# A ConvFFN's last product with one more folded pair of tiles in each half, and two of its weight sums made one stage earlier

## The chip, the cores and the metric

The kernel runs on one core of one Trainium2 chip. The metric is the device time of that core in microseconds: 1489.67 us before the change, the median of three runs that span 1489.61 to 1492.81. All traces quoted are of single executions on that core.

## What is computed

One layer of a diffusion backbone on 256 latent tokens of width 2048 and 256 context tokens: adaLN modulation, two attention branches, an output projection, and then a gated ConvFFN. The change concerns the end of it:

```python
def conv_ffn(h, w_up, conv_w, conv_b, w_down):
    u = depthwise_conv(h @ w_up, conv_w, conv_b)
    a, g = jnp.split(u, 2, axis=-1)
    return (jax.nn.silu(g) * a) @ w_down
...
y = (jax.nn.sigmoid(ga) * (oa @ w_br_a) + jax.nn.sigmoid(gb) * (ob @ w_br_b)) @ w_o
x = x + gt1 * rms_norm(y, g_attn_post[l])
h = modulate(rms_norm(x, g_ffn_pre[l]), sh2, sc2)
x = x + gt2 * rms_norm(conv_ffn(h, w_up[l], conv_w[l], conv_b[l], w_down[l]), g_ffn_post[l])
```

`w_up` is 2048 x 11264, `w_down` is 5632 x 2048: 44 tiles of 128 rows, called ff tiles below. All weights and activations are fp32.

## The kernel before

**Products.** Every fp32 product is made of three matmuls on fp32r halves: each operand is split into a high and a low part, and high·high, low·high and high·low are added in PSUM. Weights arrive by DMA in blocks of 128 x 2048 fp32 (1 MB, tiles `raw...`, a ring of four buffers, issued by SP in program order, line 154). `split` makes the high part on ScalarE (L161, tiles `wh`) and the low part, raw minus high, on VectorE (L165, tiles `wl`); each has two buffers. One such pass covers 1024 columns, so a block takes two.

**The last product** is w_down's, made in two halves `h` of 1024 output columns, each of two column blocks of 512, for two blocks of 128 tokens. Its blocks come in the order of the string `SEQ`, once per half:

- `D`, a plain block: four 128 x 512 weight tiles, each times two token blocks, three matmuls each: 24 matmuls of 128x512 (`direct`).
- `S`, a folded pair of ff tiles (`fold`). Two tiles by two column blocks by two token blocks are eight products; with sums and differences of weights and of activations seven are enough, so 21 matmuls stand for 24. The four products on sums of weights use `t0h`, `t0l`, `t1h`, `t1l`; the three on the weights themselves use `wh`, `wl`. Results that belong to several outputs stay in PSUM as x1, x5, x6, x7 and are added at the end of the half (`sums_1`, `sums_2`).

Each half has 10 D and 12 S. A fold needs, beside 0.75 MB of its own weights (loads of L204, 128x512 and 128x1024), a 1 MB tile of weight sums. `weight_sums` (L239, L241, L242) makes it in place, in three VectorE operations on a raw block. For 22 of the 24 folds this happens in the up stage, beside the w_up product: `load_sum` loads the raw block, `sum_part` sums it, and POOL's DMA queue stores the tile to DRAM (`sumd`, L279). In the last product SP loads it back (L154, `raw<-sumd`). For pair 0 of each half the fold loads its full raw block and sums it itself, beside the last product (`folded`).

**Activations.** The gated activations of plain ff tiles stay split in `ff`. Those of a folded pair are summed by `act_sums` (L263) and split into `fs`, if they are kept; for the pairs in `LATE` the unsummed activations stay in `late_a` and are summed and split anew into `late_f` in each half. The up stage ends with the evacuation of its last product (L313, L314), a three-tap convolution (L1434, L1435, L1437) and the gate (L1442, L1445).

**Wo's end.** Before the FFN, the output projection Wo runs in four column blocks c of several weight blocks g; `beside(c, g)` hangs extra work behind each. Its products are L1164, evacuation and norm sums L1173, L1174, L1245, L1250, L1251, the residual L1263.

**What sets the order.** The program is written in one order, and a scheduler places each engine's instructions in its own in-order queue; `issue_after` ties an instruction behind another one. `block(n)` splits the next block of weights and loads n blocks ahead. TensorE, VectorE, ScalarE and SP then each work through a fixed list, and wait for semaphores.

## Time and profile before

| | |
|---|---|
| median of three runs | 1489.67 us (1489.61 to 1492.81) |
| the profiled execution: its own time | 1490.08 us |
| its span in the trace | 1488.2 us, 22084 instructions |
| last product, from its first to its last matmul's start | 1255.6 to 1480.0 us |
| Wo's end (last two column blocks) | about 700 to 763 us |
| granted TensorE clock | 1.00 nearly throughout |
| bytes moved | 446.11 MB, 300 GB/s on the mean |

The span is what the trace covers; the execution's own time is 1.9 us longer, and all sums below are made on it. The chain of waits tells which engine's work the end hung on; the list of groups tells durations by the form of the operand; the list of waits and the brackets in the timeline tell what an engine stood idle for. In the timeline a row reads: start, length, engine, line, operation, out<-in, and in brackets the idle time ahead of it with what ended it.

### The profile page before, as it was taken

The page shows a single profiled execution, that of the slowest core. Times are in us where ns is not written, and L with a number is a line of the kernel's source. Part 1 is how long each engine was busy: PE and PEld are TensorE (multiplying, and loading weights), DVE is VectorE, ACT ScalarE, POOL GpSimd, SP SyncE. Part 2 cuts the span into 40 slices and gives each one's busy share as a digit, 9 for nine tenths or more (in the row PEclk, how much of TensorE's full clock was granted, in tenths as well). Part 3 has the DMA queues.
Part 4 walks back from the last instruction along what each step waited for, and adds up shares of the span by engine and source line. Part 5 has one row for each costly group of instructions (what it writes and reads, how often), then busy time and mean ns, then how long its engine had stood idle before and what let it go on. Part 6 is the DMA issues. An engine that isn't in the chain of part 4 may idle for free.

```text
span 1488.2 us, 22084 instructions
## 1 busy us (share of the span) xinstructions
PE 1478.9 (99%) x8458; PEld 1273.1 (86%) x8458; DVE 1274.5 (86%) x1961; ACT 848.8 (57%) x1405; POOL 13.6 (1%) x33
## 2 busy tenths in 40 slices
PE   9999999999999999999999999999999999999998
PEld 7877889998888888888888888888888888788886
DVE  4499878889988989899878998898999998887886
ACT  5553324777764544555766555565555555675663
POOL 0000000000000000000000000000000000000000
PEclk9999999999999999999999999999999999999999
DMA  9988699754368898986646989989889888797794
GB/s 370 394 321 340 243 387 357 268 192 170 142 237 328 340 344 310 361 325 262 236 179 235 358 338 334 337 314 354 327 310 360 328 317 290 280 323 264 275 336 200
DMA packets 73688, 446.11 MB, mean 300 GB/s; under 512 B 7904, under 2 KB 10352, under 8 KB 25328
## 3 DMA queue, kind: packets, MB, share of 16 engines
q1 hardware_dynamic: 69840, 420.85, 75.8%
q0 software_dynamic: 3168, 23.07, 3.8%
q8 instruction: 66, 1.08, 0.3%
q10 hardware_dynamic: 576, 0.80, 0.2%
q14 instruction: 38, 0.31, 0.1%
HBM read 417.37 MB, written 27.32 MB: 299 GB/s over the span
## 4 chain that ended last, share of the span: by engine, by line
PE 94%; DVE 3%; ACT 1%; DMA 1%; issue 0%; ACTq 0%; DVEq 0%
PE pu L308 21%; PE pu L309 11%; PE c L1552 9%; PE pk L589 8%; PE pv L851 7%; PE pg L308 7%; PE pq L308 4%; PE pb L308 4%; PE x L1552 4%; PE pg L309 4%; PE py_o L1164 3%; PE pq L309 2%; PE pb L309 2%; PE po L993 1%; PE s L962 1%; PE o L1092 1%
## 5 line engine op out<-in xcount | busy, mean ns | idle before, releaser
L165 DVE TENSOR_TENSOR wl<-raw,wh 128x1024 fp32r<-128x1024 f32 (+1 forms) x444 | 514.6, 1186 | 90.2 <-ACT wh L161 88.1
L161 ACT ACTIVATE wh<-raw 128x1024 fp32r<-128x1024 f32 (+1 forms) x444 | 441.4, 1027 | 193.6 <-issue 53.9
L308 PE MATMUL pu<-h,wh 128*128 128x512 f32 x1404 | 487.6, 391 | 0.0
L309 PE MATMUL pu<-h,wl 128*128 128x256 f32 x1404 | 395.9, 282 | 0.0
L308 PEld LDWEIGHTS pu<-h,wh 128*128 128x128 f32 x1404 | 263.6, 188 | 55.0
L309 PEld LDWEIGHTS pu<-h,wl 128*128 128x128 f32 x1404 | 265.5, 189 | 0.0
L308 PE MATMUL pg<-h,wh 128*128 128x512 f32 x464 | 161.5, 390 | 0.0
L309 PE MATMUL pg<-h,wl 128*128 128x256 f32 x464 | 130.9, 282 | 0.0
L313 ACT ACTIVATE half_u<-pu 128x256 f32<-128x256 f32 x88 | 33.5, 382 | 154.0 <-PE pu L309 153.9
L338 DVE SCALAR_TENSOR_TENSOR raw<-raw,crb 128x2048 f32<-128x2048 f32 x48 | 109.6, 2284 | 10.1 <-DMA raw<-in_wm_b_dram 10.1
L589 PE MATMUL pk<-h,ku 128*128 128x512 f32 x480 | 117.4, 398 | 0.3
L308 PE MATMUL pq<-h,wh 128*128 128x512 f32 x304 | 108.9, 396 | 0.1
L589 PEld LDWEIGHTS pk<-h,ku 128*128 128x128 f32 x480 | 87.6, 188 | 23.6 <-issue 3.9
L308 PEld LDWEIGHTS pg<-h,wh 128*128 128x128 f32 x464 | 87.1, 188 | 18.2
L851 PE MATMUL pv<-wh,h 128*128 128x512 f32 (+1 forms) x384 | 101.6, 354 | 0.0
L1552 PE MATMUL c<-wh,ff 128*128 128x512 f32 x320 | 98.5, 389 | 0.0
L308 PE MATMUL pb<-h,wh 128*128 128x512 f32 x256 | 89.4, 391 | 0.0
L309 PEld LDWEIGHTS pg<-h,wl 128*128 128x128 f32 x464 | 87.7, 189 | 0.0
L309 PE MATMUL pq<-h,wl 128*128 128x256 f32 x304 | 85.5, 281 | 0.0
L851 PEld LDWEIGHTS pv<-wh,h 128*128 128x128 f32 x384 | 67.7, 189 | 10.1
L309 PE MATMUL pb<-h,wl 128*128 128x256 f32 x256 | 72.1, 282 | 0.0
L1552 PEld LDWEIGHTS c<-wh,ff 128*128 128x128 f32 x320 | 60.0, 188 | 12.4
(332 smaller groups left out, 2288.4 us busy)
## 6 DMA issues: line engine op xcount, KB each, us to landing
raw<-in_ws_dram SPq DMA_DIRECT2D x222, 1024.0 KB, 6.1
raw<-in_wm_b_dram SPq DMA_DIRECT2D x64, 1024.0 KB, 5.0
sumd<-raw POOLq DMA_DIRECT2D x22, 1024.0 KB, 4.7
raw<-sumd SPq DMA_DIRECT2D x22, 1024.0 KB, 6.8
raw<-in_wm_sc_dram SPq DMA_DIRECT2D x15, 1024.0 KB, 8.2
raw<-in_ws_dram SPq DMA_DIRECT2D x22, 512.0 KB, 6.0
raw<-in_wkt_dram SPq DMA_DIRECT2D x10, 1024.0 KB, 7.6
raw<-in_wm_sh_dram SPq DMA_DIRECT2D x8, 1024.0 KB, 8.5
```

Source lines behind the costliest of these rows:

```text
L161: a_ = nc.scalar.activation(hi, src, AF.Copy)
L165: v_ = nc.vector.tensor_tensor(out=lo, in0=src, in1=hi, op=ALU.subtract)
L308: nc.tensor.matmul(pt[:, :], wh[:, w], a, start=first and i == 0, stop=False, skip_group_check=True)
L309: nc.tensor.matmul(pt[:, :S], wl[:, w], a[:, 0], start=False, stop=last and i == n - 1, skip_group_check=True)
L313: a_ = nc.scalar.activation(t[:], pt[:, S:], AF.Copy)
L338: nc.vector.scalar_tensor_tensor(out=r, in0=r, scalar=1.0, in1=row, op0=ALU.mult, op1=ALU.mult, accum_out=modx[:, j : j + 1])
L589: nc.tensor.matmul(pk[:], wt[:, w], hh[:, :, k, a], start=k == 0 and a == 0 and wt is wh, stop=k == KT - 1 and a == 1)
L851: nc.tensor.matmul(pv[i][:, :nw], src[:, k, a, t0 : t0 + P], wt[:, w], start=k == 0 and q == 0, stop=k == KT - 1 and q == 2)
L962: nc.tensor.matmul(s_ps, qs[hd][:, a, qt * P : qt * P + P], k_[:, w], start=q == 0, stop=q == 2)
L993: nc.tensor.matmul(po[:, :S], v_[:, b], pTs[hd][:, b, a], start=b == 0 and q == 0, stop=b == 3 and q == 2)
L1164: p_ = nc.tensor.matmul(py[t][:], act[:, k, a, t * P : t * P + P], wt[:, w], start=k == 0 and q == 0, stop=k == nk - 1 and q == 2)
L1552: nc.tensor.matmul(pt[:], a(i), wt[:, w], start=k not in begun, stop=stop and q == 2, skip_group_check=True)
```

## The change

The last product has 13 folded pairs and 9 plain blocks a half instead of 12 and 10. The folded pairs begin at ff tile 14 instead of 16, so 18 instead of 20 ff tiles are plain and nine instead of eight summed pairs are kept in `fs`. The string starts with D S S and has three runs of S S S a half instead of two. Since 18 plain tiles make no whole number of blocks a column block, plain blocks take their (tile, column block) entries in one running list, and the fifth block of a half holds entries of both column blocks; the host lays the weights out so.

The pair that sums its own weights is now the last of each half (`OWN`), not the first. Its three products on its own weights come ahead of the four on sums, and the splits of its sums are placed inside the fold before it. The other 24 sums are made ahead: 22 in the up stage as before, and two more at Wo's end, hung into `beside`. Pads of the tiles `wh`, `wl`, of two small tiles and a 100-column tile `rim2` shrink or go, which makes room for `fs` and `ff`.

```diff
 NE = 6
 SW = (KT - ND) * P // 4
 KW = (NKVA + NHB) * P
-J0, NS = 16, 12
-ND0 = (FT - 2 * NS) // 4
-SEQ = "DDSSDSSDSSSDSSDSSSDDDD"
-LATE = (2, 4, 7, 9)
+J0, NS = 14, 13
+SEQ = "DSSDSSSDSSSDSSSDSSDDDD"
+LATE = (2, 5, 8, 11)
+OWN = (12,)
 PO = (2, 4, 6)
 KO = [j for j in range(KT) if j // 2 * 2 not in PO]
 SEQ_O = "DSDSDSDD"
-AHEAD = [(h, p) for h in range(2) for p in range(NS) if p not in (0,)]
+AHEAD = [(h, p) for h in range(2) for p in range(NS) if p not in OWN]
 NSUM = len(AHEAD)
 SUMS_UP = [3, *range(4, FT, 2), 37]
...
         n = r.shape[-1]
         b = 1 if pool else 2
         h, lo = (
-            (pool or wp).tile([P, 2048 + 128], F32R, tag=f"w{q}", bufs=b, name=f"w{q}{nraw[0]}")[:, off : off + 2048]
+            (pool or wp).tile([P, 2064], F32R, tag=f"w{q}", bufs=b, name=f"w{q}{nraw[0]}")[:, off : off + 2048]
             for q in "hl")
         def half(q, after):
             last[:] = split(h[:, q], lo[:, q], r[:, q], after)
...
     def folded(q):
 
         h, lo = (
-            wp.tile([P, 2048 + 128], F32R, tag=f"w{c}", bufs=2, name=f"w{c}{q}")[:, :2048] for c in "hl")
+            wp.tile([P, 2064], F32R, tag=f"w{c}", bufs=2, name=f"w{c}{q}")[:, :2048] for c in "hl")
         parts[q] = (h, lo), []
         after = tuple(sum_end) if SEQ[(q - b0 - B_DN - 1) % len(SEQ)] == "S" else None
         if q in sum_of and SEQ[(q - b0 - B_DN - 1) % len(SEQ)] == "D":
...
             wsum[q] = raws[q]
             for half in range(2):
                 weight_sums(raws[q], half)
-                split_sum(q, half)
+                if SEQ[(q - b0 - B_DN - 1) % len(SEQ)] == "D":
+                    split_sum(q, half)
 
     def weight_sums(r, part):
         q = [r[:, n * 512 : n * 512 + 512] for n in range(4)]
...
 
     def folded_o(q):
         r = raws[q]
-        h, lo = (wp.tile([P, 2048 + 128], F32R, tag=f"w{c}", bufs=2, name=f"w{c}{q}")[:, :2048] for c in "hl")
+        h, lo = (wp.tile([P, 2064], F32R, tag=f"w{c}", bufs=2, name=f"w{c}{q}")[:, :2048] for c in "hl")
         for w in (slice(0, 512), slice(1024, 2048)):
             split(h[:, w], lo[:, w], r[:, w])
         ts = []
         for i, c in enumerate("hl"):
             weight_sums(r, i)
-            t = place[b0 + B_UP - 1].tile([P, 2048 + 128], F32R, tag=f"w{c}", bufs=1, name=f"t{c}{q}")
+            t = place[b0 + B_UP - 1].tile([P, 2064], F32R, tag=f"w{c}", bufs=1, name=f"t{c}{q}")
             ts.append((t[:, :1024], t[:, 1024:2048]))
             queue[q + 1] = split(*ts[i], r[:, i * 1024 : i * 1024 + 1024])
         parts[q] = (h, lo), ts
...
         def beside(c, g):
             if c == 0 and g < 2:
                 sync.dma_start(out=x1[:, g], in_=xt[:, g])
+            if (c, g) in ((1, 3), (2, 1)):
+                load_sum()
+            if (c, g) in ((2, 0), (2, 2)):
+                with tc.issue_after(last[1]):
+                    sum_part(0)
+                    sum_part(1)
             if (c, g) == (2, 3):
                 nc.vector.tensor_tensor(
                     out=modx[:, 16:48], in0=modx[:, 16:48], in1=col[:, C_BMOD + 48 : C_BMOD + 80], op=ALU.add)
...
     yp = ctx.enter_context(tc.tile_pool(name="yp2", bufs=1))
     ss = yp.tile([P, 2, 4], F32, name="ss_2")
     r = yp.tile([P, 2], F32, name="r_2")
-    yp.tile([P, 100], F32, name="rim2")
     folding.append(yp)
     x1 = fs[:].rearrange("p k a i t -> p (k a i t)")[:, : 2 * D].bitcast(F32).rearrange("p (a d) -> p a d", a=2)
...
 
     row_of(0)
     down = [j for j in range(FT) if not is_folded(j)]
+    entries = [(j, c) for c in range(2) for j in down]
+    ndir = len(entries) // 4
     for h in range(2):
         c0, c1 = 2 * h, 2 * h + 1
         cs = [slice(c * 512, c * 512 + 512) for c in (c0, c1)]
...
                     pt[:], a(i), wt[:, w], start=k not in begun, stop=stop and q == 2, skip_group_check=True)
                 begun.add(k)
 
-        def direct(wts, g, c, t):
+        def direct(wts, d, t):
             for kk in range(4):
-                j = direct_tile(down[4 * g + kk])
+                n, c = entries[4 * d + kk]
+                j = direct_tile(n)
                 product(
                     C[t, c], lambda i: ff[:, j, i, t * P : t * P + P], *wts, slice(kk * 512, kk * 512 + 512), (t, c),
-                    stop=g == ND0 - 1 and kk == 3)
+                    stop=n == down[-1])
 
         def fold(wts, p, behind=None):
             (wh, wl), (ta, tb) = wts
...
             f_ = late_f if p in LATE else fs[:, kept(p)]
             A = lambda n: lambda i: f_[:, i, n]
             end = p == NS - 1
+            def plain():
+                product(X[1], A(0), wh, wl, sl[2], 1, end)
+                product(C[0, 0], A(1), wh, wl, sl[3], (0, 0))
+                product(C[0, 1], A(6), wh, wl, sl[0], (0, 1))
+
+            if p in OWN:
+                plain()
             product(X[7], A(5), *ta, sl[0], 7, end)
             product(X[5], A(3), *ta, sl[1], 5, end)
             if behind:
...
             product(C[1, 0], A(2), *tb, sl[1], (1, 0))
             if behind:
                 split_sum(behind, 1)
-            product(X[1], A(0), wh, wl, sl[2], 1, end)
-            product(C[0, 0], A(1), wh, wl, sl[3], (0, 0))
-            product(C[0, 1], A(6), wh, wl, sl[0], (0, 1))
+            if p not in OWN:
+                plain()
 
         def late_pair(p):
             return [late_a[:, LATE.index(p), q] for q in range(2)]
...
                         late[1:] = [lambda: (sums_2(), add(C[1, 1][:], C[1, 1][:], yg[:, 1, cs[1]]))]
             else:
                 for t in range(2):
-                    direct(wts, d % ND0, d // ND0, t)
+                    direct(wts, d, t)
                 d += 1
             if h and n == 4:
                 warm_table(AF.Sqrt, "d", ss[:, 0, 0:1])
...
             late = [lambda: None, scaled]
         else:
             wts, after = [], None
-            for g in range(ND0 - lead, ND0):
+            for g in range(ndir - lead, ndir):
                 wts.append(block(3))
-                direct(wts[-1], g, 1, 0)
-                close(g - ND0 + lead, 0, 1)
+                direct(wts[-1], g, 0)
+                close(g - ndir + lead, 0, 1)
             for t in range(2):
                 if t:
-                    for i, g in enumerate(range(ND0 - lead, ND0)):
-                        direct(wts[i], g, 1, 1)
+                    for i, g in enumerate(range(ndir - lead, ndir)):
+                        direct(wts[i], g, 1)
                 close(t, 1, 1 - t, after)
                 after = finish(t)
...
     ws[B_UP + 5 : B_DN : 2] = u[FT + 2 :]
     wd = f(w_down)[0].reshape(FT, P, D)
     down = [j for j in range(FT) if not is_folded(j)]
-    d = slabs(wd[down].reshape(-1, D), 512).reshape(2, 2 * ND0, P, 2048)
+    entries = [(j, c) for c in range(2) for j in down]
     for h in range(2):
-        n, g = iter(range(2 * ND0)), iter(range(NS))
+        n, g = iter(range(0, len(entries), 4)), iter(range(NS))
         for i, kind in enumerate(SEQ):
             if kind == "D":
-                ws[B_DN + h * len(SEQ) + i] = d[h, next(n)]
+                m = next(n)
+                ws[B_DN + h * len(SEQ) + i] = np.concatenate(
+                    [wd[j][:, h * 1024 + c * 512 : h * 1024 + c * 512 + 512] for j, c in entries[m : m + 4]], axis=1)
             else:
                 j = J0 + 2 * next(g)
                 a, b = (wd[k][:, h * 1024 : h * 1024 + 1024].reshape(P, 2, 512) for k in (j, j + 1))
```

Not shown are the same smaller pads in three further functions. Lines behind the first hunk move by 1 to 15: the sums are L240, L242, L243, the product is L1560.

**VectorE at Wo's end.** `wl179` to `wl184` are the low parts of Wo's last blocks, `raw179` and `raw182` now the raw blocks of the two sums; L1251 (now L1258) is the norm's sum. Before:

```order
L1111 TENSOR_TENSOR yg_6516<-o1_1_6532,yg_6516 128x512
L1128 TENSOR_TENSOR yg_6516<-yg_6516,grow_6517 128x512
L1251 SCALAR_TENSOR_TENSOR junk2_6523,sq_6519<-yg_6516,x1_6515 128x512
L1128 TENSOR_TENSOR yg_6516<-yg_6516,grow_6517 128x512
L1251 SCALAR_TENSOR_TENSOR junk2_6523,sq_6519<-yg_6516,x1_6515 128x512
L165 TENSOR_TENSOR wl179_6886<-raw178_6799,wh179_6885 128x1024 x2
L165 TENSOR_TENSOR wl180_6918<-raw179_6845,wh180_6917 128x1024 x2
L165 TENSOR_TENSOR wl181_6950<-raw180_6891,wh181_6949 128x1024 x2
```

Now:

```order
L1129 TENSOR_TENSOR yg_6518<-yg_6518,grow_6519 128x512
L240 TENSOR_TENSOR raw179_6839<-raw179_6839 128x1024
L1258 SCALAR_TENSOR_TENSOR junk2_6525,sq_6521<-yg_6518,x1_6517 128x512
L1129 TENSOR_TENSOR yg_6518<-yg_6518,grow_6519 128x512
L242 TENSOR_TENSOR raw179_6839<-raw179_6839 128x512
L1258 SCALAR_TENSOR_TENSOR junk2_6525,sq_6521<-yg_6518,x1_6517 128x512
L243 TENSOR_TENSOR raw179_6839<-raw179_6839 128x512
L165 TENSOR_TENSOR wl180_6894<-raw178_6801,wh180_6893 128x1024 x2
L165 TENSOR_TENSOR wl182_6928<-raw180_6849,wh182_6927 128x1024 x2
L240 TENSOR_TENSOR raw182_6925<-raw182_6925 128x1024
L165 TENSOR_TENSOR wl183_6964<-raw181_6899,wh183_6963 128x1024
L242 TENSOR_TENSOR raw182_6925<-raw182_6925 128x512
```

Three operations of the first sum stand ahead of the splits of one block of Wo, and those of the second stand among the splits of another.

**ScalarE where the up stage ends and the last product begins.** `half_u` and `a` belong to the last convolution, `wh312` (before) is the second plain block, `wh189` (before) and `wh188` (now) the first folded pair. Before:

```order
L313 ACTIVATE half_u87_12012<-pu43_1_11978 128x256
L161 ACTIVATE wh312_12031<-raw311_11914 128x1024
L1434 ACTIVATE a87_12015<-u87_12011,col_67 128x256
L161 ACTIVATE wh312_12031<-raw311_11914 128x1024
L1442 ACTIVATE a87_12015<-a87_12015 128x256
L161 ACTIVATE wh189_12077<-raw312_11968 128x512
L161 ACTIVATE ff_7469<-a43_11974 128x256
L161 ACTIVATE wh189_12077<-raw312_11968 128x1024
L161 ACTIVATE t0h189_12084<-raw312_11968 128x1024
L161 ACTIVATE t1h189_12090<-raw312_11968 128x1024
```

Now:

```order
L161 ACTIVATE wh188_12057<-raw314_11937 128x512
L314 ACTIVATE half_u87_12039<-pu43_1_12005 128x256
L161 ACTIVATE wh188_12057<-raw314_11937 128x1024
L1441 ACTIVATE a87_12042<-u87_12038,col_67 128x256
L1449 ACTIVATE a87_12042<-a87_12042 128x256
L161 ACTIVATE ff_7483<-a43_12001 128x256
L161 ACTIVATE t0h188_12059<-raw313_11935 128x1024
L161 ACTIVATE t1h188_12063<-raw313_11935 128x1024
```

The second plain block is gone from this place; the folded pair's own weights are split around the last evacuation, and `t0h`, `t1h` come from another raw tile than `wh`, the one loaded from DRAM.

**VectorE at the end of a half**, where the last pair (`204`) sums its own weights (`raw341`); `wl343` is the first of the four closing plain blocks. Now:

```order
L165 TENSOR_TENSOR wl204_12718<-raw341_12664,wh204_12717 128x512
L240 TENSOR_TENSOR raw341_12664<-raw341_12664 128x1024
L165 TENSOR_TENSOR wl204_12718<-raw341_12664,wh204_12717 128x1024
L165 TENSOR_TENSOR t0l204_12733<-raw341_12664,t0h204_12732 128x1024
L242 TENSOR_TENSOR raw341_12664<-raw341_12664 128x512
L243 TENSOR_TENSOR raw341_12664<-raw341_12664 128x512
L165 TENSOR_TENSOR wl343_12758<-raw342_12691,wh343_12757 128x1024 x2
L165 TENSOR_TENSOR t1l204_12743<-raw341_12664,t1h204_12742 128x1024
```

Before, the same operations stood at the head of a half; here a plain block's two splits come between the last sum and `t1l`.

More of the change, by code (lines that the diff above doesn't have):

```diff
@@ L341, in silu_row @@
     def silu_row(pool, tag="crb", bufs=1, v=0, like=F32):
-        r = pool.tile([P, D + (0 if like == F32 else 128)], like, tag=tag, bufs=bufs, name=f"crb{v}_{nmod[0]}")
+        r = pool.tile([P, D + (0 if like == F32 else 16)], like, tag=tag, bufs=bufs, name=f"crb{v}_{nmod[0]}")
         r = r if like == F32 else r[:, :D].bitcast(F32)
@@ L347, in gain_cols @@
     def gain_cols(i, j0, g0, pool):
-        g = pool.tile([P, 120], F32, tag="gr", bufs=1, name=f"gr{i}")[:, :KT]
+        g = pool.tile([P, KT], F32, tag="gr", bufs=1, name=f"gr{i}")
         nc.vector.tensor_tensor(
@@ L551, in unit @@
                     n, raw, o = 2 * NK2 * P, ru.pop(u), 0
-                h = wp.tile([P, 2048 + 128], F32R, tag="wh", bufs=2, name=f"ku{u}")[:, 8:]
+                h = wp.tile([P, 2064], F32R, tag="wh", bufs=2, name=f"ku{u}")[:, 8:]
                 step = 2 * P if u < 2 else n
```

## The prediction

> **What bounds the kernel now.** I read the share of busy time and the chain of waits first, then the last stage by itself.
>
> ```profile
> PE 1478.9 (99%) x8458; PEld 1273.1 (86%) x8458; DVE 1274.5 (86%) x1961; ACT 848.8 (57%) x1405; POOL 13.6 (1%) x33
> PE 94%; DVE 3%; ACT 1%; DMA 1%; issue 0%; ACTq 0%; DVEq 0%
> ```
>
> TensorE is busy in all but 1488.2 − 1478.9 = 9.3 us of the span, and 94% of the chain that ended last is its own work. So only two things can move the end: the number of matmuls, and the moments in which one of them waits. DVE at 86% is an average; what counts is whether a split is late for its matmul. The last stage, by the summary of the product's line and by two pieces of the chain (start, length, what, count):
>
> ```profile
> L1552 PE MATMUL c<-wh,ff x320: 388/389/396, 1255.6 to 1479.8; 128*128 128x512 f32 x160
> L1552 PE MATMUL c<-wl,ff x160: 388/389/393, 1256.0 to 1480.0; 128*128 128x512 f32 x160
> 1297.63 2.04 PE x L1552 x9
> 1457.25 23.13 PE c L1552 x102
> ```
>
> A record is 389 ns long, but they overlap: 102 of them take 23.13 us, 9 take 2.04, so one costs 0.2267 us of TensorE. The sequence has 2 × (10 plain × 24 + 12 folded × 21) = 984 matmuls: 223.1 us. From the first start to the end of the last at this pace pass 1480.0 + 0.2 − 1255.6 = 224.6 us, so some 1.5 us of the stage is waiting. Which waits, the list of waits in this stage says (total, times, longest):
>
> ```profile
> ACT t1h L161 <- DVE raw L242: 5.2, 2, 2.6
> ACT t0h L161 <- DMA raw<-sumd: 2.7, 3, 1.5
> PEld x L1552 <- ACT t1h L161: 0.9, 2, 0.5
> PEld x L1552 <- DVE t0l L165: 0.7, 1, 0.7
> PEld x L1552 <- DVE t1l L165: 0.5, 2, 0.3
> PE x L1552 <- DVE t0l L165: 0.2, 1, 0.2
> ```
>
> The waits for t1h and t1l come twice: pair 0 sums its own weights at the head of each half, and ScalarE stands 2.6 us for that sum. The waits for t0l belong to one late load of a sum from DRAM in half 0 (the chain has 8.85 us of it, shown below). The four rows of PEld and PE add up to 2.3 us, more than the 1.5 that PE can have lost, because a weight load may wait while the array still works. I scale them to 1.5: the two own sums cost 0.9 us, 0.45 a half, and the late load 0.6.
>
> **Fewer matmuls.** 13 folded pairs and 9 plain blocks a half are 273 + 216 = 489 matmuls, before 492. Six fewer over both halves, at 0.2267 us: **−1.36 us**. That is the whole arithmetic gain, and it is certain as far as PE is the bound. The Trainium skill ("TensorE: Matmul & The Clock Gate", section "Back-to-back issue gap") has about 131 ns sustained for 512 columns and 216 ns isolated; by these the six are worth an estimated 0.79 or 1.29 us. This trace's 226.7 ns agrees with neither, and nothing below uses them.
>
> **The own sum leaves the head of a half.** Pair 0 now reads its sum from DRAM in both halves. Half 1's head: its loads can run during the four plain blocks that end half 0, which are 4 × 24 × 0.2267 = 21.8 us of cover against 6.8 us for a load (rows below). Its stall goes: **−0.4**. Half 0's head is different: the sequence now starts with D S instead of D D S, so the first fold starts 5.44 us earlier against the last up products. Rows of before at that place on ScalarE (start, length; in brackets the idle time before it and what ended it):
>
> ```profile
> 1255.81 0.38 ACT L313 ACTIVATE half_u<-pu 128x256 f32<-128x256 f32 x1 [1.02 <-PE pu L309]
> 1260.42 0.42 ACT L1442 ACTIVATE a<-a 128x256 f32<-128x256 f32 x1 [1.84 <-DVE a L1437]
> 1261.53 0.40 ACT L161 ACTIVATE ff<-a 128x256 fp32r<-128x256 f32 x1
> 1263.91 1.06 ACT L161 ACTIVATE t0h<-raw 128x1024 fp32r<-128x1024 f32 x1 [1.03 <-DVE raw L239]
> 1267.60 1.06 ACT L161 ACTIVATE t1h<-raw 128x1024 fp32r<-128x1024 f32 x1 [2.62 <-DVE raw L242]
> ```
>
> PE ends its single plain block at 1255.6 + 5.44 = 1261.0, and by the new order then has three matmuls on this pair's own weights (to 1261.7), four on t0h, one more, one on t1h, two on t0l, three on t1h, then t1l. In the new order of ScalarE t0h stands right behind the last gate's L1442 and ff. With no plain block's splits in between, the chain (each step its predecessor's end and the length of its row in this place) half_u 1256.5, u 1257.3, wl 1258.7, the convolution's two steps 1259.6, gate 1260.0, product 1260.5, ff 1260.9 gives t0h at about 1261.9, t1h 1262.9, t0l 1263.1, t1l 1264.3. Needed, if PE does not stop before: 1261.7, 1262.8, 1263.1, 1264.2. So t0h is 0.2 late and the rest then fits; the next pair's t0l (1267.4) and t1l (1268.6) are just in time. I take 0.3 us. Below that bound is 0; above, if wl and the convolution change places on VectorE (1.2 us), 1.5. Against 0.45 before: **−0.1** (−0.4 to +1.1).
>
> The late load of half 0, a row of the chain, and beside it the page's row for all loads of sums (KB each, median us to landing):
>
> ```profile
> 1276.22 8.85 DMA raw<-sumd
> ...
> raw<-sumd SPq DMA_DIRECT2D x22, 1024.0 KB, 6.8
> ```
>
> Its counterpart now is the fourth folded pair's sum, issued when the buffer of a piece split at about 1275 comes free. It lands at 1282 to 1284 for a fold that starts near 1285.7: I take 0.2 of the 0.6 away, since the load may again be up to 1 us late. **−0.2** (−0.6 to +0.4).
>
> **The own sum at the end of a half.** VectorE's work there, by the groups of the last stage (count, then busy and mean ns):
>
> ```profile
> L165 DVE TENSOR_TENSOR wl<-raw,wh 128x1024 fp32r<-128x1024 f32 x62 | 74.2, 1220 | 17.7 <-ACT wh L161 16.8 <-PE x L1552 0.8
> L165 DVE TENSOR_TENSOR t0l<-raw,t0h 128x1024 fp32r<-128x1024 f32 x24 | 29.2, 1218 | 2.3 <-ACT t0h L161 2.2
> L165 DVE TENSOR_TENSOR wl<-raw,wh 128x512 fp32r<-128x512 f32 x24 | 16.5, 688 | 11.6 <-ACT wh L161 11.6
> L239 DVE TENSOR_TENSOR raw<-raw 128x1024 f32<-128x1024 f32 x2 | 2.4, 1222 | 0.0
> L242 DVE TENSOR_TENSOR raw<-raw 128x512 f32<-128x512 f32 x2 | 1.4, 692 | 0.1
> ```
>
> One own pair is 0.69 + 1.22 (wl), 1.22 + 2 × 0.69 (sums) and 2 × 1.22 (t0l, t1l): 6.95 us, and the new order puts the next plain block's 2.44 in front of t1l. That is 9.4 us, some 9.6 with gaps, from the moment at which the pair before starts on PE and wl's buffer comes free. PE has that pair (21 matmuls), then this one's own-weight products (nine, which now go first), six on t0, four on t1h and two of the next plain block before it wants t1l: 42 × 0.2267 = 9.5 us. So t1l is at most just late: **+0.1** per half, 0.2 in all (0 to 1.0).
>
> **Two sums at Wo's end.** Per sum 1.22 + 2 × 0.69 = 2.6 us of VectorE, one load and one store. VectorE by stretches there (length, then busy of PE, PEld, DVE, ACT, POOL; clock, DMA share, GB/s), and the splits:
>
> ```profile
> 715.50:726.40 10.90, 10.90 (x50) 9.03 (x49) 9.42 (x16) 9.71 (x23) 0.00 (x0) 1.00 0.49 183
> 726.40:737.30 10.90, 10.90 (x50) 9.03 (x49) 6.19 (x6) 6.41 (x9) 0.00 (x0) 1.00 0.59 206
> 737.30:748.20 10.90, 10.90 (x50) 9.03 (x49) 8.83 (x21) 8.51 (x20) 0.00 (x0) 1.00 0.77 277
> 722.61 2.60 DVE L165 TENSOR_TENSOR wl<-raw,wh 128x1024 fp32r<-128x1024 f32 x2
> 727.32 2.36 DVE L165 TENSOR_TENSOR wl<-raw,wh 128x1024 fp32r<-128x1024 f32 x2 [2.12 <-ACT wh L161]
> 732.76 2.36 DVE L165 TENSOR_TENSOR wl<-raw,wh 128x1024 fp32r<-128x1024 f32 x2 [3.08 <-ACT wh L161]
> ```
>
> The first sum stands before the splits of 722.61: the first of the two then ends at 722.6 + 2.6 + 1.2 = 726.4, and PE begins that block at 726.26 with two matmuls on wh, so wants it at 726.7. It fits by 0.3 us. The second sum goes into the 3.08 us of idle time before 732.76, if its load has landed; VectorE works in order, so a late load also holds the splits behind it, which PE wants 4.5 us later. I take **0** (0 to +2). If that cover were gone, 5.2 us would be the price. The extra traffic is two loads and two stores of 1 MB in these 32.7 us, 4.2 MB / 32.7 us = 128 GB/s more on 183 to 277. What the queues can do at most, the view of the DMA from 690 to 765 us shows (GB/s in 40 slices):
>
> ```profile
> GB/s 424 140 61 384 393 280 4 52 363 419 385 398 74 240 310 4 184 376 0 201 358 35 354 170 74 376 197 380 175 419 101 280 245 149 406 9 0 100 428 31
> ```
>
> Up to 428, so 277 + 128 = 405 still fits, barely, and the loads of the next blocks stay ahead. POOL issues the two stores with nothing behind them but later stores; on SP the two loads push every later load of Wo by one buffer of the ring.
>
> **The rest** costs nothing: smaller pads move addresses only, the two bias loads that move earlier on SP fall into a stretch far from any wait, and the plain blocks that mix column blocks have the same 24 matmuls and the same 1 MB.
>
> Sum: −1.36 − 0.4 − 0.1 − 0.2 + 0.2 + 0 = **−1.9 us** on the profiled execution's 1490.08, so 1488.2. The median of the runs is 0.4 below that execution: I say **1487.8**.
>
> **Rivals.** (a) *Slower: the sums read from DRAM starve the third fold of a triple.* Triples S S S rise from four to six, and a D S S S group moves 6.25 MB in 87 × 0.2267 = 19.7 us, 317 GB/s, where the stage has 291 and 268 on average:
>
> ```profile
> 1255.50:1370.00 114.50, 114.21 (x502) 93.71 (x501) 93.07 (x117) 74.62 (x95) 0.00 (x0) 1.00 0.81 291
> 1370.00:1488.20 118.20, 112.31 (x489) 91.18 (x487) 93.82 (x123) 68.71 (x92) 0.00 (x0) 0.99 0.72 268
> ```
>
> In two triples ScalarE already waits for the third sum, here with the split that follows the first of them and PE's first matmuls on it:
>
> ```profile
> 1304.31 1.06 ACT L161 ACTIVATE t0h<-raw 128x1024 fp32r<-128x1024 f32 x1 [0.52 <-DMA raw<-sumd]
> 1416.46 1.06 ACT L161 ACTIVATE t0h<-raw 128x1024 fp32r<-128x1024 f32 x1 [0.66 <-DMA raw<-sumd]
> 1305.40 1.22 DVE L165 TENSOR_TENSOR t0l<-raw,t0h 128x1024 fp32r<-128x1024 f32 x1 [0.36 <-ACT t0h L161]
> 1307.15 2.04 PE x L1552 x9
> ```
>
> t0l ends at 1306.6, and PE takes it third or fifth, at 1307.4 or later: 0.8 us in hand. A load of the usual 6.8 us that takes the 8.85 seen once is 2.05 later; less the 0.8 in hand PE waits 1.25 of it. The rival decides from a load 0.8 us longer. At all six places that is 7.5 us; I price it at half of them late, 3.8: 1490.1 + 3.8 − 1.9 = 1492.0, less 0.4: 1491.6. For it: the 8.85 exists, and waits of 0.5 us are there. Against: it came once in 21 loads. Chance 0.14. (b) *The transition or Wo's end eats the gain*: S0's 1.5 instead of 0.3 and 2 at Wo's end: −1.9 + 1.2 + 2 = +1.3, 1491.0. For: VectorE's order is fixed ahead and margins are 0.2 to 0.3 us. Chance 0.15. (c) *Better: all stalls gone*, the own pair at the end and S0 free of cost, all 1.5 us of them: −1.36 − 1.5 = −2.9, 1486.8. Chance 0.17. (d) *It doesn't do what it says*: the six matmuls go, but a stall of their length takes their place, since splits and not PE set the pace of triples: VectorE has, for three folds, 3 × (0.69 + 3 × 1.22) = 13.05 us of splits, for the plain block 2.44, and for a pair summed late, by the groups
>
> ```profile
> L165 DVE TENSOR_TENSOR late_f<-asum,late_f 128x512 fp32r<-128x512 f32 x8 | 5.4, 681 | 0.0
> L263 DVE TENSOR_TENSOR asum<-late_a 128x128 f32<-128x128 f32 x16 | 3.9, 283 | 0.0
> ```
>
> and four smaller ones, about 2.4: 17.9 of 19.7 us, 91%. Close, but below: 1489.7, chance 0.09.
>
> **How the numbers follow.** The forecast has 0.45. A change under 0.3% (4.5 us) cannot be told from none here; the forecast, (b), (c) and (d) all lie inside it, and of (a) all but the case with five or six late loads, 0.04. Faster by 4.5 us would need more than the six matmuls and every stall of the stage together (2.9 us): 0.03, for what moved addresses may do, and 0.03 for the same on the other side. So slower 0.07, within 0.90. The range reaches below (c) by 0.8 us, for stalls that the list may miss, and above to (b) and (a): 1486.0 to 1491.8.
>
> **What would show it.** 6 matmuls fewer at 0.227 us in the chain. The waits of t1h for the own sum must move from the half's head to its end, and PE's waits for t1l near 1266 and 1380 must go. At the first fold PE should wait for t0h, not for t1l, by a few tenths. At Wo's end no PE wait for wl at 726 to 740. I am wrong if the end of the up stage itself moves (then it is Wo's end or the pads), or if waits of t0h for the sum's load reach PE in the triples.

## The result: 0.9% slower, and in stages that the change does not touch

The changed kernel takes 1503.65 us (median of 6 runs, 1503.39 to 1503.79); the kernel before, on the same chip, 1489.85. The ratio is 1.0089, with a 95% interval of 1.0076 to 1.0102. The forecast was 1487.8 in a range of 1486.0 to 1491.8. The profiled execution's span is 1501.6 us, 13.4 more than before.

The page of the changed kernel, shares of busy time and chain:

```profile
PE 1491.8 (99%) x8452; PEld 1268.1 (84%) x8452; DVE 1285.6 (86%) x1976; ACT 851.5 (57%) x1410; POOL 14.7 (1%) x35
PE 97%; ACT 1%; DVE 1%; DMA 1%; issue 0%; ACTq 0%
```

Six matmuls are gone, as planned, yet TensorE is busy 12.9 us longer, and its share of the chain rises from 94% to 97%. So the loss is not mainly a new wait: the matmuls themselves take longer. The table of stretches (length, then PE, PEld, DVE, ACT and POOL busy with their counts; clock, DMA share, GB/s) shows it in the middle of the up stage, 400 us in which both kernels run the same product in the same order. Before, then after:

```profile
800.00:1200.00 400.00, 400.00 (x2310) 354.64 (x2310) 366.51 (x559) 227.79 (x364) 10.25 (x19) 1.00 0.89 331
```

```profile
800.00:1200.00 400.00, 400.00 (x2292) 350.01 (x2291) 365.81 (x564) 229.16 (x369) 10.11 (x19) 1.00 0.87 324
```

In the same 400 us TensorE does 18 matmuls less, without an idle moment, at the full clock. The summary of a line gives minimum, median and maximum of one matmul's length in ns. Before, for keys and up:

```profile
L589 PE MATMUL pk<-h,ku x480: 387/389/791, 9.5 to 149.1; 128*128 128x512 f32 x160
L308 PE MATMUL pu<-h,wh x1404: 389/390/477, 766.4 to 1255.2; 128*128 128x512 f32 x176
```

After, for keys, up and the last product:

```profile
L590 PE MATMUL pk<-h,ku x480: 387/393/799, 9.2 to 150.3; 128*128 128x512 f32 x160
L309 PE MATMUL pu<-h,wh x1404: 389/394/480, 772.6 to 1265.2; 128*128 128x512 f32 x176
L1560 PE MATMUL c<-wh,ff x288: 388/393/399, 1265.5 to 1493.5; 128*128 128x512 f32 x144
```

The minima are the same; the medians go from 389 or 390 to 393 or 394, from the first product at 9 us on, long before the first instructions that the change moves (two bias loads at 165 us, before at 253 us or later). Since matmuls overlap, what counts is the distance from one start to the next ("pitch" below; worked out from all starts of a line in the trace, pauses over 300 ns left out):

```
stage (line before)        total us before   after    mean pitch of 512-column matmuls, ns
keys (L589)                   114.8          116.3        228.4 -> 231.2
values (L851)                 110.4          111.8        226.7 -> 231.3
q, gates, b, up (L308+L309)   844.4          850.4        228.6 -> 231.5
Wo (L1164)                     43.5           44.5        226.7 -> 231.7
last product (L1552)          224.65         228.45       226.9 -> 231.9
```

The last row has 984 matmuls before and 978 after. 9.9 us of the 13.4 are lost before the last product starts (1255.6, now 1265.5).

The last product has waits of its own too. After, by the list of waits:

```profile
ACT t0h L161 <- DMA raw<-sumd: 3.5, 6, 1.1
PEld x L1560 <- ACT t0h L161: 1.2, 1, 1.2
PEld x L1560 <- DVE t1l L165: 1.0, 2, 0.6
PE x L1560 <- ACT t0h L161: 0.7, 1, 0.7
PE x L1560 <- DVE t1l L165: 0.2, 1, 0.2
```

They are at the places that the prediction named, the first fold and the own pair, in place of those for the own sums at the heads of the halves.

### The profile page after: what moved, and what is told of

Same layout as the page of the kernel before. It is cut to its first block, busy times and chain, and to the rows that moved or that the text cites. A ratio compares the mean times of both kernels' runs of the same rounds, so it can differ in the third digit from the quotient of the medians.

```text
span 1501.6 us, 22116 instructions
## 1 busy us (share of the span) xinstructions
PE 1491.8 (99%) x8452; PEld 1268.1 (84%) x8452; DVE 1285.6 (86%) x1976; ACT 851.5 (57%) x1410; POOL 14.7 (1%) x35
## 4 chain that ended last, share of the span: by engine, by line
PE 97%; ACT 1%; DVE 1%; DMA 1%; issue 0%; ACTq 0%
PE pu L309 22%; PE pu L310 11%; PE c L1560 10%; PE pv L852 7%; PE pg L309 7%; PE pk L590 7%; PE x L1560 5%; PE pq L309 4%; PE pb L309 4%; PE pg L310 4%; PE py_o L1165 3%; PE o L1093 2%; PE pq L310 2%; PE pb L310 2%; PE po L994 1%; PE s L963 1%
## 5 line engine op out<-in xcount | busy, mean ns | idle before, releaser
L1560 PE MATMUL c<-wh,ff 128*128 128x512 f32 x288 | 90.1, 394 | 0.0
L852 PE MATMUL pv<-wl,h 128*128 128x512 f32 (+1 forms) x192 | 67.4, 355 | 0.0
```

Source lines behind the costliest of these rows:

```text
L852: nc.tensor.matmul(pv[i][:, :nw], src[:, k, a, t0 : t0 + P], wt[:, w], start=k == 0 and q == 0, stop=k == KT - 1 and q == 2)
L1560: nc.tensor.matmul(pt[:], a(i), wt[:, w], start=k not in begun, stop=stop and q == 2, skip_group_check=True)
```

## The experiments

In the diffs of this section `...` stands for code left out, and a line that stands for several like it says so. What the first stages have of the change is only where tiles lie in SBUF: the pads on the weight tiles went from 128 to 16 columns, so that their size is 8256 bytes, not 8704 = 17 × 512. In the kernel before, by its tiles' addresses, every large matmul has its two operands at the same byte offset modulo 512 (0 for keys and values, 480 for Wo and the last product), or the streamed activations at 0 and the stationary weights at 480 (queries, gates, up). After the change the second weight buffer lies at 32, the low parts at 96 and 160, `t0h` at 320, the activations `h` and `h2` at 256, and the key blocks in turn at 0 and 64. Theory A says that these offsets set the pace; theory B, that something in the new order, the extra sums or the extra traffic slows TensorE.

### The pads alone

```diff
-wp.tile([P, 2048 + 128], F32R, tag=f"w{q}", ...)   # all weight tiles
+wp.tile([P, 2064], F32R, tag=f"w{q}", ...)
-    yp.tile([P, 100], F32, name="rim2")             # and the two small tiles' pads, as in the change
```

> The kernel before with only the change's smaller pads: 12 folded pairs, the old order, the old sums; the addresses of the weight tiles in SBUF are as in the change (second wh tile at 32 modulo 512 bytes, wl at 96 and 160, t0h at 320) where they all were 480 or 0. Theory A (addresses set TensorE's pace): a 512-column matmul pitch of about 231 ns instead of 227 in every stage, 1502 to 1505 us. Theory B (the new order, the two sums at Wo's end or the extra loads slow TensorE): 1489.7 us, pitch 227.

Measured: 1503.43 us, ratio 1.0091 (1.0075 to 1.0106). The same stretch of the up stage:

```profile
800.00:1200.00 400.00, 400.00 (x2292) 350.00 (x2291) 363.08 (x553) 228.35 (x366) 10.24 (x19) 1.00 0.87 325
```

2292 matmuls, exactly as in the changed kernel. The pads are the whole loss; theory B falls. (Fewer bytes of pad also let the scheduler issue two bias loads earlier and swap two matmuls and two VectorE operations in the values stage, as in the change; nothing waits for the loads, and the kernels with tiles of 8192 bytes below have all of this and not the loss.)

### The change, with tiles of 8192 bytes

```diff
-wp.tile([P, 2064], F32R, tag=f"w{q}", ...)         # all weight tiles
+wp.tile([P, 2048], F32R, tag=f"w{q}", ...)
-parts[q] = halves(raws[q], 8 if q - b0 < B_Q else 0, ...)   # the key and value blocks likewise
+parts[q] = halves(raws[q], 0, ...)
+    yp.tile([P, 104], F32, name="rim2")           # and a 16-column pad of another tile goes
```

> The change with the same instructions in the same order on every engine, but tiles wh, wl of exactly 8192 bytes and two small pads, so that all operands of the large products start at 480 or 0 modulo 512 bytes again. Theory A: pitch 227, and the change's own arithmetic shows: 1486.5 to 1489, as forecast without the addresses. Theory B: stays at 1503 us.

Measured: 1494.51 us, ratio 1.0031 (1.0020 to 1.0042), with the same instructions in the same order as the change. Two thirds of the loss are back, one third not:

```profile
L590 PE MATMUL pk<-h,ku x480: 387/396/794, 9.4 to 151.3; 128*128 128x512 f32 x160
L309 PE MATMUL pu<-h,wh x1404: 389/390/476, 770.9 to 1259.7; 128*128 128x512 f32 x176
L1561 PE MATMUL c<-wh,ff x288: 388/389/395, 1260.0 to 1483.6; 128*128 128x512 f32 x144
```

Up and last product are as fast as before; keys (396) are slower than ever. The key and value blocks used to start 8 columns into their tiles, at 0 like the activations; a tile of 2048 columns has no room for that, and they now lie at 480 against 0. So what counts is not that an address is 0 or 480, since both are fine elsewhere. Keys and values are 117.1 + 112.6 us, 4.5 more than before: all of the remaining 4.5.

### Moving one operand of the up stage

```diff
+    h2p.tile([P, 120], F32, name="shift2")     # 480 bytes; in the second kernel [P, 8], 32 bytes
     h2 = h2p.tile([P, KT, 2, S], F32R, name="h2")
...
-        yp.tile([P, 64], F32, name="rim3")
+        yp.tile([P, 72], F32, name="rim3")    # in the second kernel [P, 56]
```

Only addresses change: on every engine the instructions keep the order that they have in the kernel before. The second text speaks of rule R, which was drawn from the first kernels: only the difference of the two operands' offsets counts, modulo 128 bytes.

> The kernel before with the up stage's activation tile h2 moved by 480 bytes, so that its matmuls have both operands at 480 modulo 512, not the activations at 0 and the weights at 480. Theory A1 (the two operands must have the same offset): the up stage's 1404 wide matmuls go from 228.5 to about 226.8 ns, 2.4 us faster, 1487.3. Theory A2 (each operand by itself must be near a multiple of 512): no change, 1489.7.

> The kernel before with the up stage's activation tile h2 32 bytes further, so that weights lie 64 modulo 128 behind the activations instead of 96. By R an offset that differs from the good one is bad: up stage 231 to 236 ns, 1494 to 1500 us. If instead the up stage has several good offsets (0 alone being bad): 228.5 or less, 1486 to 1490.

Measured: 1498.79 us with 480 bytes (ratio 1.0062, 1.0048 to 1.0075), 1499.32 with 32 (1.0060, 1.0046 to 1.0073). The first is the opposite of what A1 says and not what A2 says either: of the offsets tried in this stage, equal ones are the worst. The second is what R says, with 233.5 ns. Up with 480 bytes and, as a control in the same run, the gates, whose activations did not move:

```profile
L308 PE MATMUL pu<-h,wh x1404: 391/398/478, 767.0 to 1264.7; 128*128 128x512 f32 x176
L308 PE MATMUL pg<-h,wh x464: 390/390/390, 423.8 to 656.6; 128*128 128x512 f32 x155
```

The up product is built otherwise than keys, values, Wo and last product: a 512-column matmul on the high weights alternates with a 256-column one on the low weights. Its good offset is another one.

### Tiles of 8448 bytes, and of 8320

```diff
-wp.tile([P, 2048 + 128], F32R, tag=f"w{q}", ...)
+wp.tile([P, 2048 + 64], F32R, tag=f"w{q}", ...)    # 8448 bytes, in the kernel before
```

> The kernel before with tiles wh, wl of 8448 bytes instead of 8704: second buffers start at 224 modulo 512, first at 480. If addresses count modulo 256 or less: 1489.7, pitch 227. If they count modulo 512: about half of the matmuls are slow, pitch 229 on the mean, some 1496 us.

Measured: 1489.90 us, ratio 0.9999 (0.9990 to 1.0008). Offsets that differ by 256 are as good as equal ones. Then the change with tiles of 8320 bytes, 65 × 128:

```diff
-wp.tile([P, 2064], F32R, tag=f"w{q}", ...)
+wp.tile([P, 2080], F32R, tag=f"w{q}", ...)
+rim = cp.tile([P, 56], F32, name="rim"); sel = rim[:, 54:56]   # room for it, keeps all starts modulo 128
```

> The change, same instructions in the same order, with all operands of the large products at the offsets modulo 128 bytes that they have in the kernel before (weight tiles of 8320 bytes, 65 times 128, all starts at 96 modulo 128; activations h, h2 and the key and value blocks at 0). Theory R (only the difference of the two operands' offsets modulo 128 counts): pitch 226.7 in keys and values, 228.5 in the up stage, 226.8 in the last product; keys and values regain the 4.4 us that stayed lost with the tiles of 8192 bytes, so 1489 to 1490, and what is left against the kernel before is the change itself. Theory M (modulo 256 or 512 is needed): some matmuls stay at 231, 1494 to 1500 us.

Measured: 1495.94 us, ratio 1.0037 (1.0025 to 1.0050). Theory R, with modulo 128, falls for keys, values, Wo and last product: with a difference of 0 or 256 their pitch is 226.7 to 228.5 ns on the mean of a stage, with 128 or 384 it is 232.3 to 233.7, in one and the same run. The up stage keeps 229.1 and 229.4 at two differences 128 apart.

### Both operands moved together

```diff
+        hp.tile([P, 16], F32, name="shift1")                    # 64 bytes
         hh = hp.tile([P, 2, KT, 2, S], F32R, name="h")
-name=f"ku{u}")[:, 8:]          # keys; values likewise
+name=f"ku{u}")[:, 24:]
```

> The kernel before with the activation tile h and the key and value blocks all moved to 64 modulo 512. R: keys and values keep 226.7 to 228.4 ns, since both operands moved together, and only the 1024 products of h with weights at 96 (gates and queries) become slow, about 6 us, 1496. If each operand's own offset counts (0 and 96 good, 64 bad): keys and values at 231 to 234 too, 1500.

Measured: 1493.23 us, ratio 1.0020 (1.0010 to 1.0029). Keys, up and gates:

```profile
L590 PE MATMUL pk<-h,ku x480: 387/389/791, 9.3 to 149.4; 128*128 128x512 f32 x160
L308 PE MATMUL pu<-h,wh x1404: 389/390/484, 769.9 to 1258.7; 128*128 128x512 f32 x176
L308 PE MATMUL pg<-h,wh x464: 389/394/423, 424.3 to 659.3; 128*128 128x512 f32 x155
```

Keys at 64 and 64 are as fast as at 0 and 0; the gates, with one operand at 64 and the other at 480, are slow. In these streams it is the difference that counts, not either address. The slow part is smaller than expected: about 4 ns on each of the 1024, where 6 us in all were expected.

All classes together, d being the address of the stationary operand minus that of the streamed one, modulo 256; mean pitch of a stage in ns:

```
products of 512 columns after 512 (keys, values, Wo, last product), one d over a whole block
  d =   0: 226.7 to 228.8  (before, 8448 bytes, h64, 8320 bytes, part of the change's keys)
  d =  32: 233.3  (8192 bytes, values)      d =  64: 233.6  (the change, second key buffer)
  d = 128: 232.3 to 233.7  (8320 bytes)     d = 160: 233.3  (the change, products on sums)
  d = 224: 233.4  (8192 bytes, keys)
products of 512 columns alternating with 256 (queries, gates, up)
  d = 224: 228.4 to 229.6  (before, 8448, 8320 bytes, first buffer of the change)
  d =  96: 229.4  (8320 bytes, second buffer)
  d =   0: 236.1  (h2 by 480)               d =  32: 233.4  (the change, second buffer)
  d = 160: 232.6  (h64, gates)              d = 192: 233.5  (h2 by 32)
products of 512 columns after 512 in the change, where high and low parts differ in d (values, Wo, last product without sums)
  d =   0: 232.2 to 232.3                   d =  64: 230.2 to 230.5
  d = 128: 230.9 to 233.5                   d = 192: 230.2 to 230.7
```

The last group limits the rule: where d changes from one matmul to the next, a matmul's own d does not settle its pitch, and those with d = 0 are slow too.

A rival cause is the work of others. ScalarE and VectorE work on SBUF beside the matmuls, and their tiles moved as well. But in the changed kernel's up stage the matmuls of d = 32 take 233.0 ns in the 38 cases in which both engines stand idle meanwhile, and 233.6 in the 526 in which both are busy throughout. So the work of these two engines is not what slows them. DMA traffic can't be told apart so; but where only h2 moved, which the weights' transfers do not touch, only the products that read h2 became slow.

### What the change is worth without the addresses

The kernel before in the layout of the change with 8192-byte tiles:

```diff
-wp.tile([P, 2048 + 128], F32R, tag=f"w{q}", ...)   # all weight tiles, and the key and value blocks at column 0
+wp.tile([P, 2048], F32R, tag=f"w{q}", ...)
```

> The kernel before with the layout of the change with 8192-byte tiles: same offsets in every product, keys and values mismatched (their blocks at 480, activations at 0). It is the baseline on which the change differs by its own work alone. If addresses explain all that is left between that change (1494.5) and the kernel before (1490.0), this gives 1494.3 to 1495.3 with keys and values 4.4 us longer, and the change is worth 0 to -0.8 us by itself. If the change costs time beside the addresses, this stays at 1490 to 1492.

Measured: 1493.97 us, ratio 1.0026 (1.0015 to 1.0036), against 1.0031 (1.0020 to 1.0042) for the change in that layout. Spans are 1491.9 and 1491.8. By itself the change does nothing that can be measured: in the traces its last product takes 224.05 us, that of the baseline 224.19. At 0.2267 us a matmul, its 978 leave 2.3 us of waiting, the baseline's 984 only 1.1. So waits have taken the place of the six matmuls' 1.36 us. The list of waits of the change in this layout says which:

```profile
ACT t0h L161 <- DMA raw<-sumd: 2.1, 4, 0.9
PEld x L1561 <- DVE t1l L165: 1.5, 2, 0.9
PEld x L1561 <- ACT t0h L161: 1.3, 1, 1.3
PE x L1561 <- ACT t0h L161: 0.8, 1, 0.8
PE x L1561 <- DVE t1l L165: 0.6, 2, 0.5
```

From start to start, the wait for t0h at the first fold costs 1.1 us beyond the pitch, those for t1l at the ends of the two halves 0.46 and 0.73: together the 2.3.

### Two tries to win these back

First, with 8320-byte tiles, the plain block's splits tied behind the own pair's t1 split:

```diff
         parts[q][1].append(t)
+        if half and q not in sum_of:
+            queue[q + 1] = tuple(sum_end)
```

> The same, with the next plain block's splits tied behind the own pair's t1 split at the end of each half. If t1l is late because those two splits stand ahead of it on VectorE, TensorE's two waits there (0.46 and 0.73 us beyond the pitch) go and the time falls by 1.0 to 1.2 us against the kernel without the tie; if the stall only moves to the plain block's wl, no difference.

Measured: 1496.71 us, ratio 1.0042 (1.0028 to 1.0056), beside 1.0037 without the tie: no gain. The waits for t1l, and with them that of the first fold for t0h, without the tie and with it:

```profile
PEld x L1561 <- DVE t1l L165: 1.3, 2, 0.8
PE x L1561 <- ACT t0h L161: 0.8, 1, 0.8
PE x L1561 <- DVE t1l L165: 0.4, 1, 0.4
```

```profile
PEld x L1563 <- DVE t1l L165: 0.8, 2, 0.4
PE x L1563 <- ACT t0h L161: 0.8, 1, 0.8
PEld c L1563 <- DVE wl L165: 0.3, 1, 0.3
PEld c L1563 <- ACT wh L161: 0.2, 1, 0.2
```

The wait for t1l shrinks and part of it comes back on the plain block's wh and wl, which now come later. Second, thirteen pairs with the old pads, made to fit by summing a fifth pair's activations late, with two plain blocks at the head of a half and three at its end:

```diff
-SEQ = "DSSDSSSDSSSDSSSDSSDDDD"; LATE = (2, 5, 8, 11)
+SEQ = "DDSSDSSSDSSSDSSSDSSDDD"; LATE = (0, 2, 5, 8, 11)
-wp.tile([P, 2064], F32R, tag=f"w{q}", ...)
+wp.tile([P, 2048 + 128], F32R, tag=f"w{q}", ...)
-late = [sums_1, sums_2, lambda: close(0, 0, 1), lambda: close(1, 0, 1)]
+late = [sums_1, sums_2, lambda: (close(0, 0, 1), close(1, 0, 1))]   # and all closing sums at once in the second half
```

> Thirteen pairs with the old pads, so all offsets as before: the room comes from a fifth pair a half (pair 0) whose activations are summed late. The half starts with two plain blocks and ends with three. If the first fold waits 1.1 us only because one plain block is too short a cover, that wait is below 0.5 now; the six matmuls count fully: 1488.5 to 1489.5 with keys, values and up stage at their old pitch. If the late sum of pair 0 makes the first fold late instead: 1490 to 1492.

> The same with the next plain block's splits tied behind the own pair's t1 split. The waits for t1l at the ends of the halves fall from 1.0 to 0.5 us together; 0.3 to 0.6 us below the kernel without the tie, or no measurable difference.

Measured: 1490.66 us, ratio 1.0005 (0.9996 to 1.0014); with the tie 1491.33, 1.0010 (1.0001 to 1.0018). The tie shortens the two waits for t1l from 1.2 to 0.7 us in the traces, but the time does not fall with them. All old pitches are back, and so are 13 of the 13.8 us, but it does not beat the kernel before. Its waits of TensorE in the last product and the tail, without the tie:

```profile
PEld o L1529 <- ACT dg L1528: 3.0, 1, 3.0
PE o L1529 <- ACT dg L1528: 2.6, 1, 2.6
PEld x L1561 <- DVE t1l L165: 1.5, 2, 0.9
PEld x L1561 <- DVE t0l L165: 0.6, 1, 0.6
PEld c L1561 <- DVE c L1612: 0.4, 1, 0.4
```

The wait for t0h at the first fold is gone, so a second plain block is enough cover even with a late sum. But the six matmuls are lost again elsewhere. From its first to its last matmul's start the last product takes 224.4 us, as in the kernel before. Beyond the pitch the two waits for t1l still cost 0.46 and 0.73 us, a sum that lands late costs 0.5 at the third fold of a triple, and the closing plain blocks wait 0.5: 2.2 us, where the waits of the kernel before come to 1.35. Two small matmuls (L1524), which the kernel before runs behind the product, now stand inside it and take another 0.55. Then comes the tail, where VectorE has no idle time left ahead of the last results: the next matmul starts 3.0 us after the product's last one, 2.4 before. No kernel that ran is faster than the kernel before by more than the noise.

## Why the prediction was wrong

- **The step that failed** is "The rest costs nothing: smaller pads move addresses only." It was put at 0 and measures +13.4 us, in the span of the change and again alone (1503.43 against 1489.98). The prediction had addresses as a chance of 0.03 on either side, outside its range. No row of before could show the cost, since there each product has one offset throughout; but the sum multiplied everything by 0.2267 us, so an edit that might change that number had to be weighed first, or tried alone.
- **Six matmuls, −1.36**: right. 978 are left, and with the old offsets they run at 226.8 ns.
- **Half 1's head, −0.4**: right; no wait of TensorE is left there.
- **The first fold, 0.3**: mis-sized, it costs 1.1. The prediction has t0h ready 6.3 us after the product's first start; it is ready after 7.1. The chain up to ScalarE's last `ff` came 0.2 late. Most of the rest is a step that it left out: by its bracket, t0h starts only when VectorE has made the low part of that `ff`, 0.5 us later. In the changed kernel:

```profile
1270.62 0.42 ACT L161 ACTIVATE ff<-a 128x256 fp32r<-128x256 f32 x1 [0.49 <-DVE a L1452]
1271.53 1.06 ACT L161 ACTIVATE t0h<-raw 128x1024 fp32r<-128x1024 f32 x1 [0.49 <-DVE ff L165]
1272.64 1.20 PE L1560 MATMUL x<-t0h,fs 128*128 128x512 f32 x4 [0.72 <-ACT t0h L161]
```

- **The own pair at the end, 0.2**: mis-sized, 1.2 in the layout with 8192 bytes. The place was right (t1l behind the plain block's two splits), and so were VectorE's 9.4 us from its first split to the end of t1l: 9.1 in half 0, 9.4 in half 1. The sum lets them begin when the pair before starts on TensorE, in half 0 at 1340.75. But VectorE's first low part needs ScalarE's high part first, and so begins 0.7 us later in both halves. In half 0 of that layout:

```profile
1340.77 1.58 ACT L161 ACTIVATE wh<-raw 128x512 fp32r<-128x512 f32 x2 [3.11 <-PE c L1561]
1341.44 0.69 DVE L165 TENSOR_TENSOR wl<-raw,wh 128x512 fp32r<-128x512 f32 x1 [1.31 <-ACT wh L161]
1349.34 1.22 DVE L165 TENSOR_TENSOR t1l<-raw,t1h 128x1024 fp32r<-128x1024 f32 x1
```

- **The late load, −0.2**: it does not occur in the changed kernel, but there was less to gain than one trace showed. Of the seven traces with the old order, three lose 0.3 to 0.5 us at that fold and four nothing.
- **Wo's end, 0**: right. With the old offsets Wo's 192 matmuls take 43.5 us with and without the two sums, and no wait for wl is in the list.
- **Rival (a)**, starved triples: did not happen in the change. ScalarE waits for sums four to six times, up to 1.1 us, and TensorE never in a triple. But the mechanism exists. In the kernel before with h2 moved by 480 bytes the third sum of a triple came so late that TensorE lost 1.7 us (in an execution of 1500.97 us, where the median is 1498.79):

```profile
1350.51 1.06 ACT L161 ACTIVATE t0h<-raw 128x1024 fp32r<-128x1024 f32 x1 [2.88 <-DMA raw<-sumd]
```

- **Rivals (b) and (c)**: of (b) the first fold came near, 1.1 of its 1.5 us, and Wo's end cost nothing; (c) did not happen, since new waits replaced the old ones.
- **Rival (d)**, that a stall of the six matmuls' length takes their place, is what the change itself did, though not by the pace of triples: with equal offsets it is worth −0.1 us in the trace and within ±0.2% of nothing by the clock.
- **Small slips** that do not carry the result: five late loads are 6.25 − 1.9 = 4.4 us and not beyond the 4.5 that the text puts them beyond; the forecast and the rivals inside that bound have 0.96 together, not 0.90; the waits of before that it puts near 1266 stand at 1268 to 1270.

## What to carry to other kernels

When a kernel is bound by TensorE at 99%, compare the pitch of the same matmul in a stage that the edit does not touch before looking for waits: if it moved at the same granted clock, no wait in the edited stage explains it. Treat pads and offsets of matmul operands as part of the schedule: write down the difference of the two operands' addresses modulo 256 for each product, and keep it when tiles are resized. A table of matmul counts in a fixed stretch of time, such as 2310 against 2292 in 400 us, shows in one line what the busy share of 99% hides.

## What the runs showed of the hardware

The pitch of a 512-column fp32r matmul depends on where its operands lie relative to each other in SBUF. In a stream of 512-column matmuls with one difference throughout it is 226.7 to 228.8 ns when stationary and streamed operand differ by a multiple of 256 bytes, and 232 to 234 ns at the other differences tried so (32, 64, 128, 160, 224). Where the difference changes from one matmul to the next it is 230 to 233.5 ns, at a difference of 0 too (232.2). In a stream that alternates 512 and 256 columns the good differences are 96 and 224 bytes (228.4 to 229.6 ns) and the worst is 0, at 236 ns; the 256-column ones keep 117 to 120 ns throughout. A class can also slow its neighbours: in the up stage of the changed kernel the first four products on the good buffer, right after the bad one, have 230.6 to 235.8 ns, and the other twelve 228.4. Why this is so, and why the alternating stream has other good differences, stays open: no run here separates one cause from another.
